# SSD steps of a Mamba-2 / short-conv trunk: decays two half groups ahead, tiles moved between sums, spreads and products, decay subtractions behind the convolutions

## Chip, cores and metric

The kernel runs on one core of a Trainium2 chip. The metric is device time in microseconds (us), the median of several runs; lower is better. One further execution was taken with the hardware profiler, and all rows below come from it.

## What is computed

Two layers, each wrapped by two half-step SwiGLU FFNs, over 256 positions of 1024 channels. Layer 0 mixes with a Mamba-2 SSD block, layer 1 with a short convolution; an RMS norm stands before each part. The change touches the SSD block alone:

```
zxbcdt = h @ w_in                      # z 2048, x 2048, B 4x128, C 4x128, dt 32
xbc = silu(causal_dwconv(xbc, conv_w) + conv_b)      # 4 taps over x, B and C
dt = softplus(dt_raw + dt_bias); a = -exp(a_log)
a_cs = cumsum(dt * a) within chunks of 128
lmat = exp(a_cs[t] - a_cs[s]) for s <= t, else 0
y = (C B^T * lmat) @ (x * dt) + state of the chunk before, decayed
y = y + x * d_skip
g = y * silu(z)
g = g * rsqrt(mean over each of 4 groups of 512 (g*g) + eps) * norm_w
out = g @ w_out
```

All of it is float32 in and out.

## The kernel before, in words

Weights stream from HBM in units of 128 x 1024. `Weights.split` turns each unit into a high part (`whi`, a cast on ACT, L169) and a low part (`wlo`, a subtraction on DVE, L170), and TensorE multiplies high by high, high by low and low by high: three products of 256 columns for every 128 x 128 weight tile in the SSD block (`mm3`, L264 to L266). A weight unit can be used only when its cast and its subtraction are done.

The SSD block's 32 heads are worked as eight half groups of four heads, h = 0 to 7. The string `SSD_STEPS` is the program order of its steps. A letter is the kind, the digits are the half group or group and a part of it:

- `x`: one 128-channel tile of x, eight weight tiles (24 products), then a convolution (`conv_silu`: one ACT instruction L471, three DVE instructions L473) and a SiLU on ACT (L482).
- `z`: one tile of z, 24 products, then SiLU on ACT for the first six tiles (`z00` to `z21`), and for the other ten a Tanh on ACT (L640) and one DVE instruction (L641).
- `d`: the same convolution for B and C of a group; `c`: the products C B^T of a group and their mask (L577 on DVE, L582 on ACT).
- `t`: four transposes of x into PSUM (L648), multiplied by dt on DVE (L656).
- `e`: the decays of a half group: for two of its heads two Relus each on ACT (L668), for the other two two subtractions each on DVE (L670); two Exps over them on ACT (L672, L673), four more Exps for the decay from the chunk before (L677); one DVE multiplication of 128 x 1536 (L680) writes the masked matrix `mt`, which is held twice. It reads `acb`, a broadcast of a_cs loaded by a DMA that ACT issues (L621) two half groups earlier.
- `y`: the sixteen small products of a half group (L693, L698) from `mt` and t's result; then on DVE y + d x (L704) and the gate (L709 or L711), and a Square on ACT (L714, L717), added up on POOL (L718).
- `n`: the group sum (L325) and its inverse root on POOL (L330); `r`: the spread of that root over the partitions by two products (L337), then the norm (L724 on DVE, a cast L282 on ACT, L283 on DVE); `o`: 24 products with w_out into accumulators that stay in PSUM (L746 to L748).

SiLU lies in one activation table, Exp and Tanh in another; ACT loads a table (ACT_TABLE_LOAD) where the kind changes from one instruction to the next.

Program order is not issue order. The Tile framework schedules the built instructions on each engine by its own estimate of times, and the result is fixed when the kernel is built: each engine runs its list strictly in order. `behind(i, first)` adds an edge without a semaphore, so that the scheduler puts `i` after `first`. PSUM tiles of the tag `ps` (all single tiles of x, z, t, y, c, n and r) share four buffers; which tile takes which buffer is also fixed at the build, and the first product into a buffer waits until the tile before it in that buffer has been read.

Of the kernel before, what the change touches and what calls it, by code (L numbers as in the profile page):

```python
# [13 lines left out]
AF = mybir.ActivationFunctionType  # L14
ALU = mybir.AluOpType
# [25 lines left out]
def tile_order():  # L41
# [62 lines left out]

SSD_STEPS = (
# [4 lines left out]
).split()  # L110
SILU_TILES = 6
RELU_HEADS = 2
# [78 lines left out]
def trunk(ctx: ExitStack, tc: tile.TileContext, xT, flat, par, cst, fin, out):  # L191
    nc = tc.nc
    vec, act, pe = nc.vector, nc.scalar, nc.tensor
# [29 lines left out]
    def c(i):  # L223
        return pr[:, i : i + 1]
# [13 lines left out]
    def sb(tag, shape, bufs=2, dt=F32):  # L238
        return tmp.tile(shape, dt, tag=tag, name=nm(tag), bufs=bufs)

    def behind(i, first):

        if first is not None:
            tc.add_manual_dep(
                i.ins, first.ins.name,
                mybir.DependencyInfo(mybir.DependencyClass.NoSync, mybir.DependencyReason.DATA),
                reason="order",
            )
        return i
# [207 lines left out]
    def ssd(nxt):  # L457
# [6 lines left out]
        def conv_silu(dst, u, ct):  # L464

            a = sb("u2", [P, T], 3)

            def w(k):
                return c(C_CW + ct * 4 + k)

            act.activation(a, u, AF.Identity, bias=c(C_CB + ct), scale=w(3))  # L471
            for sh in (1, 2, 3):
                vec.scalar_tensor_tensor(  # L473
                    a[:, sh:], u[:, : T - sh], w(3 - sh), a[:, sh:], op0=ALU.mult, op1=ALU.add
                )
            silu(dst, a)


        exps, silus = [], []

        def silu(dst, src):
            silus.append(behind(act.activation(dst, src, AF.Silu), exps[0] if exps else None))  # L482
# [21 lines left out]
        def bc_conv(g):  # L504
            conv_silu(bT[g], raw[g][:, 0], 16 + g)
            conv_silu(cT[g], raw[g][:, 1], 20 + g)
# [112 lines left out]
        def bcast(h):  # L619
            a = acb[h] = sb("acb", [P, 4, T], 2)  # L620
            nc.scalar.dma_start(a, decays[1][4 * h : 4 * h + 4].partition_broadcast(P))  # L621

        def do_x(h, e):
            if e == 0:
                xh[h] = big.tile([P, 2, T], F32, tag="blk", name=nm("xs"), bufs=KF)
            ps = single()
            run(mm3, [(ps[:, :T], "ssd_in", DI + (2 * h + e) * P)], KD, xn)
            conv_silu(xh[h][:, e], ps[:, :T], 2 * h + e)
# [29 lines left out]
        def do_e(h):  # L658

            g = h // 2  # L660
            a, acs = acb[h], decays[0]
            e = mt[h] = sb("mt", [P, 4, 3, P], 2)
            for q in range(4):
                hd = 4 * h + q
                for ch in range(2):
                    aq, eq, bias = a[:, q, ch * P : (ch + 1) * P], e[:, q, 2 * ch], acs[:, ch, hd : hd + 1]
                    if q < RELU_HEADS:
                        act.activation(eq, aq, AF.Relu, bias=bias, scale=-1.0)  # L668
                    else:
                        vec.tensor_scalar(eq, aq, bias, 0.0, op0=ALU.subtract, op1=ALU.min)  # L670
            r = RELU_HEADS
            behind(act.activation(e[:, :r, 0:3:2], e[:, :r, 0:3:2], AF.Exp, scale=-1.0), silus[-1])  # L672
            behind(act.activation(e[:, r:, 0:3:2], e[:, r:, 0:3:2], AF.Exp), silus[-1])  # L673
            for q in range(4):
                hd = 4 * h + q
                behind(
                    act.activation(e[:, q, 1], a[:, q, P:], AF.Exp, bias=acs[:, 2, hd : hd + 1]),  # L677
                    silus[-1],
                )
            vec.tensor_mul(e, e, cbm[g].unsqueeze(1).broadcast_to([P, 4, 3, P]))  # L680
            if h + 2 < 8:
                bcast(h + 2)
# [56 lines left out]
        def do_o(g, q):  # L739
# [15 lines left out]

        todo = {
            "x": do_x, "z": do_z, "t": do_t, "e": do_e, "p": do_p, "b": do_b, "y": do_y, "n": do_n, "r": group_norm,
            "c": cb_path, "d": bc_conv, "o": do_o,
        }
# [42 lines left out]
    for m in range(KD):  # L802
        if m < 4:
            W.split()
        feed(m, 0, sq=False)
    ffn(0, 0, 1)
    ssd(2)
    ffn(0, 1, 3)
    ffn(1, 0, 4)
# [64 lines left out]
```

## Time and profile before

| | before |
|---|---|
| median of 3 runs | 1050.86 us (1050.17 to 1051.79) |
| the profiled execution's own time | 1051.06 us |
| its span, first to last instruction | 1048.9 us |
| mean granted TensorE clock | 0.998 |
| TensorE busy | 1035.6 us, 99% |
| VectorE (DVE) busy | 782.0 us, 75% |
| ScalarE (ACT) busy | 615.5 us, 59% |
| GpSimd (POOL) busy | 34.2 us, 3% |

A share of busy time is an average over the whole span. The SSD steps run from about 225 to 395 us; the rest is FFNs and the short convolution. What an engine waits for is shown as an idle time and the instruction that ended it.

### The profile page before, as it was taken

How to read it: one execution, taken by the hardware profiler on the slowest of the kernel's cores; microseconds unless marked ns; L12 is line 12 of the kernel's file. 1: busy time of each engine (PE TensorE's matmuls, PEld its weight loads, DVE VectorE, ACT ScalarE, POOL GpSimd, SP SyncE). 2: the span in 40 equal slices, each digit the busy share in tenths (PEclk: the TensorE clock that was granted, in tenths of full speed). 3: DMA queues.
4: the chain of work that ended last, by engine and by line, in shares of the span. 5: the costliest groups of instructions: out<-in, count | busy, mean ns of one | idle time of the engine just before them, and what ended most of it. 6: DMA issues, size and time to landing. Idle time of an engine off the chain costs nothing.

```text
span 1048.9 us, 16814 instructions
## 1 busy us (share of the span) xinstructions
PE 1035.6 (99%) x6468; PEld 921.4 (88%) x6468; DVE 782.0 (75%) x1176; ACT 615.5 (59%) x985; POOL 34.2 (3%) x41
## 2 busy tenths in 40 slices
PE   8999999999999999999999999999999999999997
PEld 6888888899989898888888888888899988888886
DVE  6977766689898878777766777776667788777643
ACT  7655554567688557555544655554454476555543
POOL 0000000130022200000000000000000000000000
PEclk9999999999999999999999999999999999999999
DMA  8655665556555446666555665566555556665661
GB/s 275 219 186 178 197 187 186 172 172 192 183 199 182 148 154 182 190 190 182 184 194 183 181 186 192 185 183 192 187 174 187 182 181 185 188 190 177 198 198 55
DMA packets 55135, 192.96 MB, mean 184 GB/s; under 512 B 6128, under 2 KB 7696, under 8 KB 55056
## 3 DMA queue, kind: packets, MB, share of 16 engines
q1 hardware_dynamic: 53568, 187.15, 57.6%
q10 hardware_dynamic: 1488, 4.75, 1.3%
q8 instruction: 50, 0.82, 0.3%
q14 instruction: 29, 0.24, 0.1%
HBM read 190.80 MB, written 1.08 MB: 183 GB/s over the span
## 4 chain that ended last, share of the span: by engine, by line
PE 96%; DVE 1%; DMA 1%; ACT 1%; issue 0%; SPq 0%; POOL 0%; POOLq 0%; ACTq 0%; DVEq 0%
PE pp L257 31%; PE pp L259 14%; PE ps L257 13%; PE ps L259 6%; PE ps L264 5%; PE ps L265 5%; PE ps L266 5%; PE pp L256 2%; PE ps L414 2%; PE ps L415 2%; PE ps L413 2%; PE pp L746 1%; PE pp L748 1%; PE pp L747 1%; PE pp L266 1%; PE pp L264 1%
## 5 line engine op out<-in xcount | busy, mean ns | idle before, releaser
L170 DVE TENSOR_TENSOR wlo<-raw,whi 128x1024 fp32r<-128x1024 f32 (+2 forms) x361 | 432.1, 1199 | 186.4 <-ACT whi L169 180.1
L169 ACT CAST whi<-raw 128x1024 fp32r<-128x1024 f32 (+2 forms) x361 | 370.5, 1028 | 325.0 <-issue 98.9
L257 PE MATMUL pp<-xhl,whi 128*128 128x512 f32 x1408 | 485.9, 398 | 2.7 <-DVE xhl L295 1.8
L259 PE MATMUL pp<-xhl,wlo 128*128 128x256 f32 x1232 | 346.5, 281 | 0.2
L257 PEld LDWEIGHTS pp<-xhl,whi 128*128 128x128 f32 x1408 | 253.2, 188 | 52.2 <-DVE xhl L295 3.2
L259 PEld LDWEIGHTS pp<-xhl,wlo 128*128 128x128 f32 x1232 | 232.8, 189 | 9.3 <-DVE wlo L170 1.6
L257 PE MATMUL ps<-ac,whi 128*128 128x512 f32 x528 | 185.2, 399 | 0.0
L259 PE MATMUL ps<-ac,wlo 128*128 128x256 f32 x504 | 141.5, 281 | 0.0
L257 PEld LDWEIGHTS ps<-ac,whi 128*128 128x128 f32 x528 | 97.8, 188 | 22.4
L259 PEld LDWEIGHTS ps<-ac,wlo 128*128 128x128 f32 x504 | 95.2, 189 | 1.1
L370 DVE TENSOR_TENSOR t2b<-pp,t2a 128x512 f32<-128x512 f32 x88 | 60.4, 686 | 18.6 <-ACT t2a L370 18.6
L264 PE MATMUL ps<-xn,whi 128*128 128x256 f32 x256 | 73.8, 288 | 0.3 <-DVE u L473 0.3
L265 PE MATMUL ps<-xn,whi 128*128 128x256 f32 x256 | 72.4, 283 | 0.0
L266 PE MATMUL ps<-xn,wlo 128*128 128x256 f32 x256 | 72.4, 283 | 0.0
L370 ACT COPY t2a<-pp 128x512 f32<-128x512 f32 x88 | 51.1, 581 | 32.5 <-PE pp L257 32.5
L378 DVE TENSOR_TENSOR t2b<-t2b,inv 128x512 f32<-128x512 f32 x88 | 60.1, 684 | 0.1
L264 PE MATMUL ps<-xhl,whi 128*128 128x256 f32 x192 | 54.4, 284 | 0.2 <-ACT u L777 0.2
L265 PE MATMUL ps<-xhl,whi 128*128 128x256 f32 x192 | 54.3, 283 | 0.0
L266 PE MATMUL ps<-xhl,wlo 128*128 128x256 f32 x192 | 54.3, 283 | 0.0
L264 PEld LDWEIGHTS ps<-xn,whi 128*128 128x128 f32 x256 | 49.0, 191 | 1.4 <-issue 1.2
L256 PE MATMUL pp<-xhl,wlo 128*128 128x256 f32 x176 | 49.7, 282 | 0.0
L265 PEld LDWEIGHTS ps<-xn,whi 128*128 128x128 f32 x256 | 49.0, 192 | 0.0
(175 smaller groups left out, 1328.6 us busy)
## 6 DMA issues: line engine op xcount, KB each, us to landing
raw<-flat SPq DMA_DIRECT2D x347, 512.0 KB, 3.6
acb<-ad ACTq DMA_DIRECT2D x8, 512.0 KB, 4.6
raw<-flat SPq DMA_DIRECT2D x5, 256.0 KB, 3.1
raw<-flat SPq DMA_DIRECT2D x8, 128.0 KB, 4.1
x<-xT SPq DMA_DIRECT2D x3, 256.0 KB, 5.4
fw<-fin SPq DMA_DIRECT2D x2, 256.0 KB, 4.4
out<-y SPq DMA_DIRECT2D x2, 256.0 KB, 2.0
out<-y ACTq DMA_DIRECT2D x2, 256.0 KB, 2.5
```

Source lines behind the costliest of these rows:

```text
L169: self.nc.scalar.copy(hi[:, :w], r[:, :w])
L170: self.nc.vector.tensor_sub(lo[:, :w], r[:, :w], hi[:, :w].bitcast(F32))
L256: pe.matmul(ps[:, :T], lo, xs[:, 0], start=False, stop=False)
L257: pe.matmul(ps, hi, xs.rearrange("p a t -> p (a t)"), start=first, stop=last)
L259: pe.matmul(ps[:, :T], lo, xs[:, 0], start=False, stop=False)
L264: pe.matmul(ps, hi, xs[:, 0], start=first, stop=False)
L265: pe.matmul(ps, hi, xs[:, 1], start=False, stop=False)
L266: trail.append(pe.matmul(ps, lo, xs[:, 0], start=False, stop=last))
L370: first = act.copy(pb, pp[:, :, T:]), vec.tensor_add(s, pp[:, :, :T], pb)
L378: vec.tensor_mul(s, s, both(inv))
L413: pe.matmul(ps[b], xh, hi, start=False, stop=False)
L414: pe.matmul(ps[b], xh, lo, start=False, stop=False)
```

## The change

A new order of the steps in `SSD_STEPS`, and two further edges for the scheduler. In the string, `e1` stands ahead of `c3`, `e2` ahead of `t2`, and so on, each decay step some tiles earlier than before; `z` and `o` tiles stand between `n` and `r`, and between `r` and `o`, in another way. In the code, the Relus of the decays are put behind the SiLU that was last in program order, and the DVE subtractions behind the convolution that was last in program order (`convs` records the last tap of each).

```
-    "c2 x60 x61 e0 x70 x71 c3 z20 z21 e1 y0 t2 z30 y1 z31 t3 e2 z40 z41 e3 n0 y2 z50 r0 y3 e4 t4 "
-    "o00 z51 t5 e5 o01 o02 o03 n1 y4 t6 z60 r1 e6 z61 y5 t7 z70 e7 y6 z71 o10 o11 n2 o12 y7 o13 r2 "
-    "o20 n3 o21 o22 r3 o23 o30 o31 o32 o33"
+    "c2 x60 x61 e0 x70 x71 e1 c3 z20 z21 y0 e2 t2 z30 y1 e3 t3 z31 z40 y2 e4 n0 t4 z41 z50 y3 e5 r0 "
+    "t5 z51 o00 o01 n1 y4 e6 t6 z60 o02 r1 o03 z61 y5 e7 t7 z70 o10 y6 n2 z71 o11 r2 y7 o12 o13 o20 "
+    "n3 o21 r3 o22 o23 o30 o31 o32 o33"
...
             for sh in (1, 2, 3):
-                vec.scalar_tensor_tensor(
+                i = vec.scalar_tensor_tensor(
                     a[:, sh:], u[:, : T - sh], w(3 - sh), a[:, sh:], op0=ALU.mult, op1=ALU.add
                 )
+            convs.append(i)
             silu(dst, a)
...
-        exps, silus = [], []
+        exps, silus, convs = [], [], []
...
                     if q < RELU_HEADS:
-                        act.activation(eq, aq, AF.Relu, bias=bias, scale=-1.0)
+                        behind(act.activation(eq, aq, AF.Relu, bias=bias, scale=-1.0), silus[-1])
                     else:
-                        vec.tensor_scalar(eq, aq, bias, 0.0, op0=ALU.subtract, op1=ALU.min)
+                        behind(
+                            vec.tensor_scalar(eq, aq, bias, 0.0, op0=ALU.subtract, op1=ALU.min),
+                            convs[-1],
+                        )
```

What the build makes of it is seen in the fixed lists of the engines. Lines after L680 of the changed kernel stand 4 lower than in the one before (L669 is the Relu, L672 the subtraction, L676, L677 and L681 the Exps, L684 the multiplication, L697 and L702 y's products, L708, L713 and L715 y + d x and the gate).

First place: ACT, from the last SiLUs of z to the decays of half group 1 (`mt_288` before, `mt_284` now) and, now, of half group 2 (`mt_295`). Before:

```order
L482 ACTIVATE zs_285_3243<-ps_286_3244 128x256
L169 CAST whi106_3297<-raw106_3127 128x1024
L482 ACTIVATE xs_279_3163<-u2_283_3232 128x256
L482 ACTIVATE zs_285_3243<-ps_287_3276 128x256
L672 ACT_TABLE_LOAD
L672 ACTIVATE mt_288_3308<-mt_288_3308 128x2x2x128
L673 ACTIVATE mt_288_3308<-mt_288_3308 128x2x2x128
L677 ACTIVATE mt_288_3308<-acb_232_2544,acs_225_2469 128x128 x4
L714 ACTIVATE gsq_292_3338<-zs_226_2471 128x256
L621 DMA acb_289_3324<-ad_2467 128x1024
L717 ACTIVATE sq_294_3343<-zs_226_2471 128x256
```

And in the change:

```order
L483 ACTIVATE xs_279_3163<-u2_283_3232 128x256
L669 ACTIVATE mt_284_3238<-acb_232_2544,acs_225_2469 128x128 x4
L677 ACT_TABLE_LOAD
L677 ACTIVATE mt_284_3238<-mt_284_3238 128x2x2x128
L676 ACTIVATE mt_284_3238<-mt_284_3238 128x2x2x128
L681 ACTIVATE mt_284_3238<-acb_232_2544,acs_225_2469 128x128 x4
L483 ACT_TABLE_LOAD
L483 ACTIVATE zs_287_3261<-ps_289_3294 128x256
L622 DMA acb_285_3254<-ad_2467 128x1024
L718 ACTIVATE gsq_292_3338<-zs_226_2471 128x256
L721 ACTIVATE sq_294_3343<-zs_226_2471 128x256
L669 ACTIVATE mt_295_3346<-acb_278_3161,acs_225_2469 128x128 x4
```

The four Relus of half group 1 now stand directly ahead of its table load (before, they stood some 60 rows earlier, among the convolutions); the same holds for half group 0. The last SiLU of z now comes after these Exps, with a table load of its own, and the row that follows the ones shown is the table load for half group 2. The whole list has 17 table loads where it had 15.

Second place: TensorE, from y of half group 2 (`ps_316`) to the tile z41 (`ps_327`), with the semaphores that each row waits for. In the change:

```order
L702 MATMUL ps_316_3521<-mt_295_3346,t2a_298_3369 64x128 x2
L325 MATMUL ps_323_3559<-ones_94,gsq_292_3338 128x2 [waits DVE_49,Pool_49]
L325 MATMUL ps_323_3559<-ones_94,gsq_292_3338 128x2
L649 MATMUL ps_325_3565<-cs_74,xs_259_2877 128x128 [waits DVE_49,PE_49]
L649 MATMUL ps_325_3565<-cs_74,xs_259_2877 128x128 x3
L264 MATMUL ps_327_3572<-xn_187_2197,whi107_3393 128x256 [waits DVE_49]
```

Before, y of half group 2 (`ps_320`) was followed by a whole z tile:

```order
L325 MATMUL ps_318_3555<-ones_94,gsq_292_3338 128x2
L693 MATMUL ps_320_3561<-mt_309_3450,t2a_296_3351 64x256 [waits DVE_49]
L693 MATMUL ps_320_3561<-mt_309_3450,t2a_296_3351 64x256 [waits Activation_49]
L698 MATMUL ps_320_3561<-mt_309_3450,t2a_296_3351 64x128 x2
L693 MATMUL ps_320_3561<-mt_309_3450,t2a_296_3351 64x256 [waits Activation_49] x2
L698 MATMUL ps_320_3561<-mt_309_3450,t2a_296_3351 64x128 x2
L264 MATMUL ps_326_3582<-xn_187_2197,whi108_3430 128x256 [waits DVE_49]
```

In the change the transposes t4 (`ps_325`) are put into the PSUM buffer that y of half group 2 has just filled, and z41 (`ps_327`) into the buffer of t4; so each of the two waits for DVE. The same pattern comes again one half group later: y of half group 3 (`ps_332`), the spread r0 (`ps_339`), the transposes t5 (`ps_348`) in y's buffer, and z51 (`ps_350`) in the buffer of z41.

Third place: DVE in the change, what stands between the reads of the first two of those buffers, y's `ps_316` and t4's `ps_325`:

```order
L708 SCALAR_TENSOR_TENSOR u4_319_3535<-xs_241_2669,pr_73,ps_316_3521 128x256 [waits DVE_49]
L713 TENSOR_TENSOR zs_287_3261<-u4_317_3530,zs_287_3261 128x256 [waits DVE_49]
L713 TENSOR_TENSOR zs_287_3261<-u4_319_3535,zs_287_3261 128x256 [waits DVE_49]
L672 TENSOR_SCALAR mt_321_3541<-acb_296_3362,acs_225_2469 128x128 [waits DMAHW4_49]
L672 TENSOR_SCALAR mt_321_3541<-acb_296_3362,acs_225_2469 128x128 x3
L657 TENSOR_TENSOR t2a_326_3570<-ps_325_3565,dt5_201_2225 128x512 [waits PE_49]
```

And between the reads of the next two, y's `ps_332` and z41's `ps_327`:

```order
L708 SCALAR_TENSOR_TENSOR u4_333_3650<-xs_244_2707,pr_73,ps_332_3641 128x256 [waits DVE_49,PE_49]
L684 TENSOR_TENSOR mt_321_3541<-mt_321_3541,cbm2_175_2031 128x1536 [waits DVE_49,Activation_49]
L715 SCALAR_TENSOR_TENSOR zs_299_3371<-u4_333_3650,zs_299_3371 128x256 [waits DVE_49]
L708 SCALAR_TENSOR_TENSOR u4_335_3656<-xs_244_2707,pr_73,ps_332_3641 128x256
L170 TENSOR_TENSOR wlo110_3594<-raw110_3313,whi110_3593 128x1024 [waits DMAHW1_49,Activation_49]
L642 SCALAR_TENSOR_TENSOR zs_313_3486<-u3_328_3603,ps_327_3572 128x256 [waits Activation_49]
```

So the product of t4's result waits behind two gates and four subtractions, and the second read of y of half group 3 behind the multiplication of half group 4 and a gate.

## Rows read from the trace of the kernel before

**Rows 1.** The page, busy time: engine, us (share of the span), instructions.
```profile
PE 1035.6 (99%) x6468; PEld 921.4 (88%) x6468; DVE 782.0 (75%) x1176; ACT 615.5 (59%) x985; POOL 34.2 (3%) x41
```
**Rows 2.** Waits of TensorE from 225 to 395 us: us in total, times, longest.
```profile
PE ps L693 <- DVE mt L680: 1.7, 2, 1.0
PE ps L337 <- POOL tv L330: 1.1, 1, 1.1
PE pp L746 <- DVE x L753: 0.4, 1, 0.4
PE ps L264 <- DVE u L473: 0.3, 1, 0.3
```
**Rows 3.** Windows: us; PE, PEld, DVE, ACT, POOL busy; granted clock, DMA share, GB/s.
```profile
260.00:283.00 23.00, 23.00 (x193) 22.95 (x192) 19.75 (x34) 14.36 (x24) 0.00 (x0) 1.00 0.58 175
283.00:295.00 12.00, 12.00 (x104) 11.35 (x103) 9.98 (x16) 11.94 (x23) 0.00 (x0) 1.00 0.51 167
300.00:318.00 18.00, 17.34 (x153) 16.33 (x152) 16.56 (x34) 14.69 (x37) 4.73 (x4) 1.00 0.53 185
```
**Rows 4.** Timeline of ACT: start, us, instruction, count, [idle before it].
```profile
283.08 0.41 ACT L482 ACTIVATE xs<-u 128x256 f32<-128x256 f32 x1
283.49 1.28 ACT L672 ACT_TABLE_LOAD   x1
284.79 0.63 ACT L672 ACTIVATE mt<-mt 128x512 f32<-128x512 f32 x1
...
287.12 1.28 ACT L482 ACT_TABLE_LOAD   x1
...
291.81 0.39 ACT L482 ACTIVATE zs<-ps 128x256 f32<-128x256 f32 x1
292.21 1.28 ACT L672 ACT_TABLE_LOAD   x1
...
294.56 1.27 ACT L677 ACTIVATE mt<-acb,acs 128x128 f32<-128x128 f32 x4
...
298.70 1.28 ACT L668 ACTIVATE mt<-acb,acs 128x128 f32<-128x128 f32 x4
299.88 0.62 ACT L673 ACTIVATE mt<-mt 128x512 f32<-128x512 f32 x1
```
**Rows 5.** Timeline of TensorE around y of half group 1 (L693 at 297.70).
```profile
293.13 0.66 PE L648 MATMUL ps<-cs,xs 128*128 128x128 f32 x4
293.54 0.37 PE L264 MATMUL ps<-xn,whi 128*128 128x256 f32 x1
...
297.70 0.65 PE L693 MATMUL ps<-mt,t2a 128*64 128x256 f32 x4 [1.04 <-DVE mt L680]
...
299.15 0.39 PE L264 MATMUL ps<-xn,whi 128*128 128x256 f32 x1
```
**Rows 6.** Timeline of DVE in the stretch of half groups 0 to 3.
```profile
295.89 1.75 DVE L680 TENSOR_TENSOR mt<-mt,cbm 128x1536 f32<-128x1536 f32 x1
...
302.76 0.69 DVE L656 TENSOR_TENSOR t2a<-ps,dt 128x512 f32<-128x512 f32 x1 [0.38 <-PE ps L648]
...
305.76 1.22 DVE L170 TENSOR_TENSOR wlo<-raw,whi 128x1024 fp32r<-128x1024 f32 x1
306.89 0.41 DVE L641 SCALAR_TENSOR_TENSOR zs<-u,ps 128x256 f32<-128x256 f32 x1
...
310.31 0.87 DVE L704 SCALAR_TENSOR_TENSOR u<-xs,pr,ps 128x256 f32<-128x256 f32 x2 [0.97 <-PE ps L698]
311.10 0.75 DVE L709 TENSOR_TENSOR zs<-u,zs 128x256 f32<-128x256 f32 x2
311.77 0.87 DVE L670 TENSOR_SCALAR mt<-acb,acs 128x128 f32<-128x128 f32 x4
```
**Rows 7.** Groups by line, POOL's additions: count | busy us, mean ns | idle before.
```profile
L718 POOL TENSOR_TENSOR gsq<-gsq,sq 128x256 f32<-128x256 f32 x12 | 16.2, 1350 | 105.7 <-ACT sq L717 105.3
```
**Rows 8.** Timeline of DVE, the first subtractions of the decays.
```profile
236.08 0.87 DVE L670 TENSOR_SCALAR mt<-acb,acs 128x128 f32<-128x128 f32 x4 [4.32 <-DMA acb<-ad]
```

## Prediction

> **What bounds the kernel now.** I read the page's busy times first: TensorE is busy 1035.6 of 1048.9 us [rows 1], so a change of order can only take away idle time of TensorE, or add some. Next come TensorE's waits in the SSD stretch: y waits twice for the decay multiplication L680, 1.7 us in all, 1.04 of it before y of half group 1 [rows 2, 5]; a spread waits 1.1 us for POOL; a product waits 0.3 us for a convolution; the 0.4 us at the block's end is not touched. So the most that the order can give back here is 1.7 + 1.1 + 0.3 = 3.1 us. Third, the windows by stage, for what the waits wait for: from 283 to 295 us ACT is busy 11.94 of 12.00 us, where DVE still has 2 us free; from 260 to 283 us ACT had 8.6 us free [rows 3]. ACT is idle 41% of the whole span [rows 1], yet in these 12 us it is the engine that sets the decays. The granted clock is 1.00 in all three windows, which is the level of 2.4 GHz.
>
> **The change, step by step.** Durations are those of the profiled execution, whose own time is 1051.06 us, 0.2 above the median.
>
> *Decay subtractions behind the convolutions.* Before, the first four subtractions held DVE until their broadcast had landed, 4.32 us of idle time [rows 8], and convolutions queued behind them; the product that waited 0.3 us [rows 2] stands there. Now that queue is clear: -0.3.
>
> *y of half group 1.* The Exps of half groups 0 and 1 keep their places behind x, but eight Relus that stood among the convolutions now stand right ahead of them on ACT, where nothing is free. Four Relus hold ACT for 1.18 us, from 298.70 to 299.88 [rows 4]; two sets are 2.36. One SiLU of z moves behind the Exps, which gives 0.40 (291.81 to 292.21 [rows 4]). So the last Exp ends at 295.83 + 1.96 = 297.8 (295.83 is 294.56 + 1.27 [rows 4]), the multiplication of 1.75 us [rows 6] at 299.6, and y starts at about 299.7 where it started at 297.70. TensorE gets there at 296.66 as before, since y, t2 and z30 precede it in both orders [rows 5]. The wait grows from 1.04 to 3.0: **+2.0**.
>
> *y of half group 2.* From 297.8 ACT works off: a table load of 1.28 back to SiLU, that SiLU (0.3), two Squares and a DMA issue (1.0, an estimate from the 0.39 of the SiLU), four Relus 1.18, a load of 1.28, and Exps of 2.33 (284.79 to 287.12) [rows 4]. That ends at 305.2 and its multiplication at 307.0. TensorE gets there at 299.7 + 1.45 (y, 297.70 to 299.15) + 0.41 (transposes, 293.13 to 293.54) + 24 and then 20 products of 0.12, or 306.8 (a tile of 24 products lies between 293.54 and 296.66) [rows 5]. So y waits 0.2. The next weight unit's cast stands behind the same Exps and its subtraction behind the multiplication, ready at 307.0 + 1.1 = 308.1, about 0.3 later than wanted: **+0.5** together.
>
> *y2, t4 and z41 in one buffer.* t4 cannot start before both reads of y, 0.87 us [rows 6], and only the two tiny sums of n0 (some 0.4) are left for TensorE meanwhile: 0.5. Then z41 waits for the product of t4's result, which stands behind two gates and four subtractions: from 311.10 to 312.55 such a row of six took 1.45 us, and the product itself 0.69 [rows 6]. That is 2.1 us from t4's start, less 0.41 for the transposes themselves: 1.7. Together **+2.1** with rounding.
>
> *y3, t5 and z51.* DVE reads y3 in two halves with the multiplication of half group 4 and a gate between them: 0.39 + 1.67 + 0.33 + 0.47 = 2.9 us [rows 6], less some 0.4 of spread products: 2.5. z51 then waits for the read of z41, which stands behind a weight subtraction: 1.13 + 0.41 [rows 6], less 0.41 of transposes: 1.1. **+3.6**.
>
> *The bounds of these two.* Before shows no such buffer wait, so the 5.7 us are worked out from other rows. From below: if TensorE reaches y later than I reckon, more of DVE's queue is done, and half of it goes, 2.9. From above: a row of DVE that waits for ACT in between adds one cast, about 1 us, to each. I take the sums of the rows, since the list on DVE is fixed and every row in it has a measured duration.
>
> *POOL.* The sums n0, n1 and n3 now come close behind the last Square. An addition on POOL lasts 1.35 us in the mean [rows 7]; each sum waits for between none and one of them, so 0 to 4.0 in all. I take **+0.8**, near the lower end, because a whole y or o stands between most of them.
>
> *Waits that go.* The 0.7 us left of the y waits was y3's, now reckoned above with its buffer, and the 1.1 us at the last spread goes, since 24 products now lie between n3 and r3: -1.8. DMA traffic, weight units and the number of products are the same, so nothing else moves.
>
> **The sum.** -0.3 + 2.0 + 0.5 + 2.1 + 3.6 + 0.8 - 1.8 = +6.9 on 1051.06, and 0.2 less for the median: **1057.7 us**.
>
> On the table loads, a row first: ACT begins the next instruction 1.30 us after a load's start (283.49 to 284.79), and the load begins the moment the one before ends (283.08 + 0.41) [rows 4]; so the two added loads are 2.6 us of ACT. The Trainium skill ("ScalarE: Activation LUTs", section "What ACT_TABLE_LOAD costs") has a drain of about 1.38 us beside the load of 1.28, so two added switches would hold ACT 5.3 us, y of half group 2 would come 2.8 us later, and the sum would be 1060.5. The rows show no such drain, so I leave it out.
>
> **Rivals.**
>
> *The decays do come early enough (faster).* If the multiplication of half group 1 ended by 296.66, when TensorE arrives, and the buffers were read in time, the 3.1 us of waits would go: 1047.8. For it: ACT is idle 41% of the span, and the steps are named earlier. Against it: by the rows the multiplication ends at 299.6, 3 us past that point, because the Relus moved to where ACT is full. Chance 0.04.
>
> *The buffer waits are mostly hidden.* ACT is late as forecast, but TensorE, held up once, finds DVE done. Then 4.5 or more of the 5.7 us go: 1053. Against it: a wait inside one buffer starts from y's own end, however late that is. Chance 0.13.
>
> *The order changes nothing that counts.* The waits that go and those that come would have to cancel within 2 us, which needs both the ACT term and one buffer chain to fail. Chance 0.05.
>
> *The clock falls.* The wait before y of half group 1 becomes 3.0 us, three times the longest of this stretch [rows 2]. If TensorE dropped to its level of 1.2 GHz until y of half group 2, up to 7.3 us of work would take up to twice as long; half of that is +3.6: 1061.3. The rows have 1.00 around waits of about 1 us and nothing longer, so they cannot exclude it. Chance 0.06. The Trainium skill ("TensorE: Matmul & The Clock Gate", section "HAM oscillation — how this bites in real kernels") says that idle gaps between products bring the clock back to its lower level; no row here shows it.
>
> **How the numbers follow.** The forecast has 0.72. About 0.2%, or 2 us, is what a measurement of this kernel can tell from no change. The range is 1053.5 to 1061.5: the low end is the sum with half of the buffer waits and none at POOL (6.9 - 2.9 - 0.8 = +3.2), a little lower to take in part of the hidden-buffer case; the high end adds POOL's upper bound (+3.2) and covers the clock's middle. Faster by over 0.2%: 0.04; within: 0.05; slower: 0.91.
>
> **What would show it.** Right: a wait of some 3 us before y of half group 1, ended by L684; 17 table loads; TensorE waiting for DVE before t4, z41, t5 and z51, 0.5, 1.7, 2.5 and 1.1 us; ACT full from 283 to about 318 us; the wait of the last spread gone; everything after the block as before, only later. Wrong: a wait under 2 us before that y says that the Relus cost nothing there; no waits at the transposes says that the buffers were free.

## The result, and the profile after

The changed kernel takes 1058.97 us (median of 4 runs, 1058.57 to 1059.41). The kernel before, run beside it, takes 1051.13 us (1050.17 to 1051.79). The ratio is 1.006, with a 95% interval of 1.0036 to 1.0084: slower, beyond the 0.2% that a measurement can tell. The two medians are 7.8 us apart (0.75%, inside the interval). The profiled run took 1058.84 us with a span of 1056.4 us, 7.5 more than before. The page's busy times of the changed kernel, which answer to [rows 1]:

```profile
PE 1037.9 (98%) x6468; PEld 922.6 (87%) x6468; DVE 782.8 (74%) x1176; ACT 618.4 (59%) x987; POOL 35.0 (3%) x41
```

The same 6468 products are made. ACT has two instructions more, the two table loads. Of the 7.5 us, 5.2 are more idle time of TensorE and 2.3 longer busy time (1037.9 less 1035.6). TensorE's waits from 225 to 405 us in the changed kernel (us in total, times, longest), which answer to [rows 2]; the 0.4 us at the block's end, as before, is left out:

```profile
PE ps L697 <- DVE mt L684: 3.2, 1, 3.2
PE ps L649 <- DVE u L708: 2.9, 2, 2.4
PE ps L264 <- DVE t2a L657: 1.3, 1, 1.3
PE ps L264 <- DVE zs L642: 0.7, 1, 0.7
```

And in TensorE's timeline of the changed kernel (start, us, instruction, count, idle time before it and who ended it): y of half group 1, t4, z41, t5, z51.

```profile
298.85 0.65 PE L697 MATMUL ps<-mt,t2a 128*64 128x256 f32 x4 [3.21 <-DVE mt L684]
...
310.14 0.63 PE L649 MATMUL ps<-cs,xs 128*128 128x128 f32 x4 [0.52 <-DVE u L708]
...
312.11 0.39 PE L264 MATMUL ps<-xn,whi 128*128 128x256 f32 x1 [1.34 <-DVE t2a L657]
...
323.05 0.63 PE L649 MATMUL ps<-cs,xs 128*128 128x128 f32 x4 [2.43 <-DVE u L708]
324.42 0.39 PE L264 MATMUL ps<-xn,whi 128*128 128x256 f32 x1 [0.75 <-DVE zs L642]
...
325.15 0.41 PE L265 MATMUL ps<-xn,whi 128*128 128x256 f32 x1
325.37 0.41 PE L266 MATMUL ps<-xn,wlo 128*128 128x256 f32 x1
...
328.53 0.28 PE L264 MATMUL ps<-xn,whi 128*128 128x256 f32 x1
328.65 0.28 PE L265 MATMUL ps<-xn,whi 128*128 128x256 f32 x1
```

All five waits stand where the prediction put them; the ones that it had before y of half group 2 and at POOL's sums are not there. The last four rows show something else: products that came every 0.12 us come every 0.21 us for a while. The windows of that stretch say why (us; PE, PEld, DVE, ACT, POOL busy; granted clock, DMA share, GB/s):

```profile
322.00:324.00 2.00, 0.63 (x4) 0.42 (x4) 2.00 (x5) 1.40 (x5) 0.83 (x1) 1.00 0.00 0
324.00:326.00 2.00, 1.58 (x8) 1.58 (x9) 2.00 (x5) 1.01 (x3) 0.63 (x1) 0.70 0.42 78
326.00:328.00 2.00, 2.00 (x11) 2.00 (x11) 2.00 (x9) 1.53 (x5) 0.74 (x1) 0.50 0.81 223
```

TensorE's clock fell to 0.50, its level of 1.2 GHz, after the waits before t5 and z51. Fifteen products from 324.94 to 328.14 us took 3.20 us instead of 1.80, a loss of 1.4 us. The sum of the rows is +2.17 (3.21 instead of 1.04) + 5.04 (the four waits) + 1.4 (clock) - 2.1 (the waits of 0.3, 0.7 and 1.1 us that went) = +6.5 of the 7.5 us. The last 1.0 us is for the most part two products that start only when DVE has made the low part (`wlo`) of their weight unit. The two subtractions in DVE's timeline, and the two products in TensorE's with the one before the second:

```profile
305.73 1.77 DVE L170 TENSOR_TENSOR wlo<-raw,whi 128x1024 fp32r<-128x1024 f32 x1
307.56 0.39 PE L266 MATMUL ps<-xn,wlo 128*128 128x256 f32 x1
...
313.64 1.22 DVE L170 TENSOR_TENSOR wlo<-raw,whi 128x1024 fp32r<-128x1024 f32 x1
314.49 0.28 PE L265 MATMUL ps<-xn,whi 128*128 128x256 f32 x1
314.91 0.39 PE L266 MATMUL ps<-xn,wlo 128*128 128x256 f32 x1
```

The subtractions end at 307.50 and 314.86, and the products start 0.06 and 0.05 us later; the second stands 0.42 us behind the product before it, where 0.12 is the usual step. That makes 0.3 to 0.4 us for each, an estimate. Such short waits stand in no list of waits above.

Rows that name an instruction as the end of a wait do not tell why it came so late, nor whether the parts add up. The experiments ask that.

### The profile page after: what moved, and what is told of

The parts are those of the page before. It is cut to its first block, busy times and chain, and to the rows that moved or that the text cites. A ratio compares the mean times of both kernels' runs of the same rounds, so it can differ in the third digit from the quotient of the medians.

```text
span 1056.4 us, 16828 instructions
## 1 busy us (share of the span) xinstructions
PE 1037.9 (98%) x6468; PEld 922.6 (87%) x6468; DVE 782.8 (74%) x1176; ACT 618.4 (59%) x987; POOL 35.0 (3%) x41
## 4 chain that ended last, share of the span: by engine, by line
PE 93%; ACT 3%; DVE 1%; DMA 1%; issue 1%; SPq 0%; POOL 0%; ACTq 0%; DVEq 0%; POOLq 0%
PE pp L257 31%; PE pp L259 14%; PE ps L257 13%; PE ps L259 6%; PE ps L264 5%; PE ps L266 5%; PE ps L265 4%; PE pp L256 2%; PE ps L415 2%; PE ps L413 2%; PE ps L414 2%; PE pp L750 1%; PE pp L751 1%; PE pp L752 1%; PE pp L266 1%
## 5 line engine op out<-in xcount | busy, mean ns | idle before, releaser
L259 PE MATMUL pp<-xhl,wlo 128*128 128x256 f32 x1232 | 346.5, 281 | 0.4 <-DVE wlo L170 0.2
L266 PEld LDWEIGHTS ps<-xn,wlo 128*128 128x128 f32 x256 | 49.7, 194 | 0.9 <-DVE wlo L170 0.9
```

The costliest lines, as they stand in the source:

```text
L259: pe.matmul(ps[:, :T], lo, xs[:, 0], start=False, stop=False)
L266: trail.append(pe.matmul(ps, lo, xs[:, 0], start=False, stop=last))
```

## The experiments

**Theory A** is the prediction's: the Relus on a full ACT, and buffers shared between a y and the tile behind it, are prices of their own that add up. **Theory B** says that the decays, named two half groups ahead, put DVE's list in the wrong order, and that the shared buffers are only where TensorE meets that. Further rivals stand in the expectations. All times are medians, and each ratio is to runs of the kernel before on the same chip.

### The order alone, and the edges alone

```diff
 (order_only: the changed kernel, and)
-behind(act.activation(eq, aq, AF.Relu, bias=bias, scale=-1.0), silus[-1])
+act.activation(eq, aq, AF.Relu, bias=bias, scale=-1.0)
-behind(vec.tensor_scalar(eq, aq, bias, 0.0, op0=ALU.subtract, op1=ALU.min), convs[-1])
+vec.tensor_scalar(eq, aq, bias, 0.0, op0=ALU.subtract, op1=ALU.min)
 (edges_only: both edges, and the SSD_STEPS of the kernel before)
```

> The new order of steps with none of the new edges. Theory A (the parts of the changed kernel's loss add up: y of half group 1 +2.2, the four waits before t4, z41, t5 and z51 +5.0, the lower clock after them +1.5, a late weight unit +0.3, waits that went -2.1): without the edge on the Relus they stand among the convolutions again, so the wait before y of half group 1 falls from 3.2 to 1.0 to 1.3 us and the rest stays; 1051.1 + 0.2 + 5.0 + 1.5 + 0.3 - 1.8 = 1056.3, and the clock still falls after z51. Rival C (the loss is the Relu edge's, since ACT is full there and all that comes later is late because of it): 1050 to 1052, and the waits before t4, z41, t5 and z51 shrink with the one before y of half group 1.

> The old order of steps with both new edges. Theory A: the wait before y of half group 1 is about 3.3 us (eight Relus now on a full ACT; it was 1.04), the 0.3 us before a product goes, and the two waits of the group sums and the spread in the last quarter (0.7 and 1.1) stay; no shared buffers, clock 1.00 throughout; 1051.1 + 2.3 - 0.3 = 1053.1, less whatever of y3's 0.7 us the delay takes up: 1052.4 to 1053.1. Rival C (the edge is the whole loss): 1057 to 1059. Rival D (the edge costs nothing, since the scheduler finds the Relus another place): 1050.5 to 1051.3.

The order alone took 1058.3 us (1.0067, 1.0049 to 1.0084), 2 us over what theory A gave. The wait before y of half group 1 was 1.3 us as expected and the four others were as in the changed kernel, but the median is only 0.7 us lower than the changed kernel's (the profiled runs, 1057.4 and 1058.84, are 1.4 apart). The clock fell here too, to 0.55 and 0.60 from 322 to 326 us. This kernel also lacks the edge of the convolutions, which is tried by itself below.

The edges alone took 1052.86 us (1.0008, 0.9996 to 1.002), the time that theory A gave, but not in its way: the clock, which was to stay at 1.00, fell. TensorE's timeline of that run has the longer wait, and products every 0.21 us behind it:

```profile
299.31 0.65 PE L697 MATMUL ps<-mt,t2a 128*64 128x256 f32 x4 [3.37 <-DVE mt L684]
...
301.60 0.41 PE L265 MATMUL ps<-xn,whi 128*128 128x256 f32 x1
301.81 0.41 PE L266 MATMUL ps<-xn,wlo 128*128 128x256 f32 x1
```

Of its 12 runs, eleven have a mean granted clock of 0.996 to 0.998 and take 1052.1 to 1054.1 us; one has 1.000 and takes 1050.56. So a fall of the clock goes with about 2.3 us here (1052.86 less 1050.56), an estimate that rests on that one run; it has no trace, so whether its wait was as long is not known. The waits of y3 and of a product (0.7 and 0.3 us) have gone from the traced run. Rival C, which wanted 1050 to 1052 for the order and 1057 to 1059 for the edges, is out: by the medians the order costs 7.2 us by itself, the edges 1.8 (the interval of their ratio takes in 1), and both together 7.8.

### The four tiles in buffers of their own

```diff
-            pt = single()
+            pt = pair()[:, 0] if h in (4, 5) else single()
...
-            py = single()
+            py = pair()[:, 0] if h in (2, 3) else single()
```

> The changed kernel, but y of half groups 2 and 3 and the transposes t4 and t5 get the four PSUM banks that the output accumulators take up only later, so none of the four shares a buffer with the tile behind it. Theory A: the four waits go (-5.0) and with them the fall of the clock (-1.5): 1059.0 - 6.5 = 1052.5. Rival B (DVE is behind by then, because the decays' multiplications stand earlier in its list, and the shared buffer is only where TensorE happens to meet that): nothing is gained, 1057 to 1059; the same 4 to 6 us stand before y of half group 3, before a product that reads a wlo (L170), or before the first products of o, and DVE's list ends the stretch at the same time as in the changed kernel.

1063.9 us (1.0116, 1.0099 to 1.0133): nothing was gained, 5 us were lost. TensorE's waits in this run:

```profile
PE ps L697 <- DVE mt L684: 3.2, 1, 3.2
PE ps L266 <- DVE wlo L170: 2.3, 1, 2.3
PE pp L751 <- DVE gn L283: 2.3, 1, 2.3
PE pp L697 <- DVE mt L684: 1.3, 1, 1.3
PE ps L697 <- DVE zs L642: 0.4, 1, 0.4
```

No transposes wait any more, but TensorE waits for the next things that DVE owes: a weight unit, the norm of r0, the decays of half group 3. That is 6.3 us behind y of half group 1, where the changed kernel had 5.04. Theory A's second part falls. The clock was low twice here, at 0.51 and 0.64 from 300 to 304 us and at 0.50 to 0.83 from 326 to 338; the changed kernel has one short fall. So some 1.3 of the 5 us are waits, and the rest goes with the clock (an estimate, the difference of the two): shared buffers or not, the waits for DVE come to much the same.

### The last third of the order alone

```diff
 ... y3 e4 t4 o00 z51 t5 e5 o01
-o02 o03 n1 y4 t6 z60 r1 e6 z61 y5 t7 z70 e7 y6 z71 o10 o11 n2 o12 y7 o13 r2 o20 n3 o21 o22 r3 o23
+n1 y4 e6 t6 z60 o02 r1 o03 z61 y5 e7 t7 z70 o10 y6 n2 z71 o11 r2 y7 o12 o13 o20 n3 o21 r3 o22 o23
```

> The kernel before, with the new order only from n1 on (half groups 4 to 7 and the output tiles between the sums, spreads and norms), without the edges. Theory A and rival B alike: the waits of the last quarter (0.7 before a group sum or y, 1.1 before the last spread) fall to 0.3 or less and nothing is added, 1051.1 - 1.5 = 1049.6, so the gain of the change was real and was in the string's last third. Rival E (those two waits only move to the sums, which now come close behind the last addition on POOL): 1050.8 to 1051.5.

1055.19 us (1.0039, 1.0025 to 1.0052), with runs from 1052.64 to 1059.93. Both expectations missed on the slow side. The profiled run is the fastest of them, so what the others add to it is in no trace. TensorE waits three times for POOL, 3.3 us, 2.6 of it before n2 (its row in TensorE's timeline):

```profile
352.24 0.61 PE L325 MATMUL ps<-ones,gsq 128*128 128x2 f32 x4 [2.61 <-POOL gsq L718]
```

The two additions that n2 waits for took POOL 5.03 us, where the same two took 1.56 in the changed kernel. POOL's rows of this run and of the changed kernel, one line each:

```profile
347.16 5.03 POOL L718 TENSOR_TENSOR gsq<-gsq,sq 128x256 f32<-128x256 f32 x2 [14.85 <-ACT sq L717]
```

```profile
353.31 1.56 POOL L722 TENSOR_TENSOR gsq<-gsq,sq 128x256 f32<-128x256 f32 x2 [10.99 <-ACT sq L721]
```

So the wait of 1.1 us before the last spread, which went in the changed kernel, was not a gain of this part of the order by itself: here it goes too, but 3.3 us of waits for POOL take its place. In the changed kernel POOL has the time: its two additions start 5.1 us before n2's products (353.31 and 358.44), here only 2.5 us before TensorE is ready for them (347.16, and 352.24 less 2.61). Why the Squares come sooner there is not shown. A delay of TensorE by itself is not enough: edges_back, below, is held up for 3.37 us before y of half group 1 and still waits 1.9 us for POOL at two sums. One reason why runs of such kernels lie far apart is shown next.

### The decays back, and the decays alone

```diff
 (decays_back: order_only with e1 to e5 one half group ahead, as before)
-e1 c3 z20 z21 y0 e2 t2 z30 y1 e3 t3 z31 z40 y2 e4 n0 t4 z41 z50 y3 e5 r0 t5 z51 o00
+c3 z20 z21 e1 y0 t2 z30 y1 e2 t3 z31 z40 e3 y2 n0 t4 z41 z50 y3 e4 r0 t5 z51 e5 o00
 (decays_early: the kernel before with e1 to e5 two half groups ahead)
-c3 z20 z21 e1 y0 t2 z30 y1 z31 t3 e2 z40 z41 e3 n0 y2 z50 r0 y3 e4 t4 o00 z51 t5 e5
+e1 c3 z20 z21 y0 e2 t2 z30 y1 e3 z31 t3 z40 z41 n0 y2 e4 z50 r0 y3 e5 t4 o00 z51 t5
```

> The new order without the new edges (as in order_only), but with the decay steps e1 to e5 back behind the tiles where the kernel before has them, one half group ahead instead of two. In the built lists t4, z41, t5 and z51 then each get a buffer of their own. Theory B, now sharper (the decays two half groups ahead put a multiplication of 1.75 us and its wait for ACT ahead of the reads, gates and weight subtractions that TensorE needs next; all else in the new order is harmless): the wait of y3's read and all four waits before t4, z41, t5 and z51 go, the clock stays at 1.00 between 320 and 330 us, and what is left are y of half group 1 (1.0) and some waits of sums for POOL (1 to 3, as in tail_alone): 1050 to 1053, from 1058.3. Rival F (the tiles of z and the transposes, moved between the y steps, are the cause): 1056 to 1059, with the same four waits.

> The kernel before, where only the decay steps e1 to e5 are moved to the places that they have in the change; all other steps and the code as before. Theory B: DVE and ACT get behind as in the change, TensorE waits 3 to 6 us more between 300 and 330 us, at a product that reads a wlo (L170), at the first product of o or at a z tile, and perhaps a second or two of lower clock behind it: 1054 to 1058. Rival F: nothing but a shift of waits, 1050.5 to 1052.

With the decays back, the new order takes 1053.77 us (1.0025, 1.0011 to 1.004) instead of 1058.3. The decays alone, moved early in the old order, take 1056.51 us (1.0046, 1.003 to 1.0063), 5.5 us over the kernel before on the same chip; TensorE waits there 1.9 us for the read of a z tile and 1.9 us for weight subtractions, and the clock is at 0.50 from 322 to 324 us. Theory B forecast the second; the first lies 0.8 us over its upper end. The waits before t4, t5 and z51 are gone as it said, and the clock is at 1.00 from 320 to 330 us, but z41 still waits 1.02 us for DVE's read of a z tile. Rival F missed both. DVE's waits of the changed kernel from 300 to 330 us, and then those of decays_back from 300 to 335, show what is different:

```profile
DVE u L708 <- PE ps L702: 6.2, 3, 3.2
DVE mt L684 <- ACT mt L681: 0.7, 1, 0.7
```

```profile
DVE wlo L170 <- ACT whi L169: 1.0, 1, 1.0
DVE mt L680 <- ACT mt L677: 0.6, 1, 0.6
DVE u L704 <- PE ps L698: 0.5, 1, 0.5
```

In the changed kernel DVE itself stands idle for 6.2 us, for y. It is not too slow; its list is in the wrong order. DVE's timeline around y of half group 3 in the changed kernel:

```profile
320.03 0.48 DVE L708 SCALAR_TENSOR_TENSOR u<-xs,pr,ps 128x256 f32<-128x256 f32 x1 [3.16 <-PE ps L702]
320.43 1.75 DVE L684 TENSOR_TENSOR mt<-mt,cbm 128x1536 f32<-128x1536 f32 x1
322.09 0.42 DVE L715 SCALAR_TENSOR_TENSOR zs<-u,zs 128x256 f32<-128x256 f32 x1
322.43 0.47 DVE L708 SCALAR_TENSOR_TENSOR u<-xs,pr,ps 128x256 f32<-128x256 f32 x1
322.82 1.22 DVE L170 TENSOR_TENSOR wlo<-raw,whi 128x1024 fp32r<-128x1024 f32 x1
```

And in decays_back:

```profile
317.79 1.22 DVE L170 TENSOR_TENSOR wlo<-raw,whi 128x1024 fp32r<-128x1024 f32 x1
...
319.26 1.22 DVE L170 TENSOR_TENSOR wlo<-raw,whi 128x1024 fp32r<-128x1024 f32 x1
...
320.84 0.87 DVE L704 SCALAR_TENSOR_TENSOR u<-xs,pr,ps 128x256 f32<-128x256 f32 x2
```

With late decays, DVE splits the next weight units while TensorE is still busy, and is there when y is done; TensorE has tiles to go on with. With early decays, the read of y stands ahead of the weight units, so DVE waits 3.16 us for TensorE. Then the multiplication of a half group that is not needed yet (1.75 us) goes ahead of the second read and the weight unit, and TensorE waits for DVE. Each engine idles in turn.

The runs of decays_back lie between 1051.68 and 1058.81 us; the profiled one took 1056.56 and shows one reason; no other run of this kernel has a trace. Before DVE's first subtraction, and before the product behind it:

```profile
239.11 0.87 DVE L670 TENSOR_SCALAR mt<-acb,acs 128x128 f32<-128x128 f32 x4 [7.57 <-DMA acb<-ad]
```

```profile
242.57 0.36 PE L264 MATMUL ps<-xn,whi 128*128 128x256 f32 x1 [3.55 <-DVE u L473]
```

The row of the kernel before has 4.32 us [rows 8], and 0.3 us of a product's wait; the traces of order_only, tail_alone and decays_early have 4.2 to 4.4 us. So the broadcast's DMA landed some 3 us later in this run than in the four others, and all that DVE has behind that subtraction waited with it.

### The edge of the convolutions

```diff
 (back_conv: decays_back, and)
 (conv_edge: the kernel before, and)
-vec.tensor_scalar(eq, aq, bias, 0.0, op0=ALU.subtract, op1=ALU.min)
+behind(vec.tensor_scalar(eq, aq, bias, 0.0, op0=ALU.subtract, op1=ALU.min), convs[-1])
```

> As decays_back, and with the change's edge of the subtractions behind the convolutions (not the one of the Relus). Theory B: the edge takes away the 0.3 us before one product and may bring the read of z31 or z40 forward by up to 1.5 us, so 0.3 to 1.5 us under decays_back. Rival G (the edge does nothing): the same time as decays_back within 0.5 us.

> The kernel before with the edge of the subtractions behind the convolutions alone. Theory H (in the kernel before, DVE's first subtraction stands ahead of convolutions and waits 4.3 us for the broadcast by DMA, 7.6 us in the profile of decays_back, where a product then waited 3.5 us; how late that DMA lands differs from run to run): the idle time of L672 for the DMA goes, the median falls by no more than 0.7 us, to 1050.2 to 1051.0, and no run lies over 1053, while the kernel before has runs to 1056. Rival: the scatter has another cause and stays, with runs of 1054 to 1056.

back_conv takes 1051.08 us (0.9998, 0.9987 to 1.0009), 2.7 under decays_back: more than theory B's 1.5, and rival G is out. conv_edge takes 1050.35 us (0.9978, 0.9964 to 0.9992), faster than the kernel before by 0.22%, which is just more than can be told from no change; the medians are 1.4 us apart (1051.78 before), twice the fall of 0.7 that theory H allowed, though the time lies in its range. Its twelve runs lie between 1049.61 and 1051.06; of the 29 runs of the kernel before beside it (1050.39 to 1057.86), 11 lie over 1053. None does with the edge, as theory H had it; its rival is out. DVE's wait for the broadcast is gone from its trace; its first wait of that stretch, at 232.90 us, is 1.71 us for ACT's part of a convolution.

So one of the two edges is a gain, and the whole change hides it.

### The edge of the Relus

```diff
 (relu_free: the changed kernel, and)
-behind(act.activation(eq, aq, AF.Relu, bias=bias, scale=-1.0), silus[-1])
+act.activation(eq, aq, AF.Relu, bias=bias, scale=-1.0)
 (edges_back: the changed kernel, and the steps of decays_back)
```

> The changed kernel without the edge of the Relus; its order of steps and the edge of the subtractions stay. Theory A (the parts add up): the wait before y of half group 1 falls from 3.2 to about 1 us and the time by 2.2, to 1056.8. Theory B (DVE is behind for its decays anyway, so a TensorE that comes 2 us earlier to y of half groups 2 and 3 waits the longer there): under 1 us of gain, 1058.0 to 1059.0, and 1 to 2 us more than in the changed kernel before t4, z41, t5 and z51 or in lower clock.

> The changed kernel with both edges, and only the decay steps e1 to e5 back behind the tiles where the kernel before has them. Theory B: of the loss of 7.8 us only the wait before y of half group 1 (3.3 us, part of it taken up by y of later half groups) and a fall of the clock behind it stay, as in edges_only, which took 1.8 us more than the kernel before: 1051.1 + 1.8 = 1052.9, with 1051 to 1054 as the bounds (no fall of the clock; a wait of n1 for POOL besides). Theory A (the early decays are not what matters): 1057 to 1059.

relu_free takes 1058.3 us (1.0059, 1.0037 to 1.008): 0.7 us of gain for 2.4 us less of wait (3.2 to 0.8). The time is theory B's, but not its reason: the four waits grew only from 5.04 to 5.22 us. What took the gain is the clock, which fell twice in this run, at z51 as in the changed kernel and also after the waits of 0.52 and 1.33 us before t4 and z41. The windows of relu_free:

```profile
308.00:310.00 2.00, 1.01 (x7) 1.01 (x8) 2.00 (x4) 2.00 (x8) 0.77 (x1) 0.93 0.60 201
310.00:312.00 2.00, 2.00 (x11) 2.00 (x10) 2.00 (x4) 2.00 (x7) 2.00 (x1) 0.50 0.04 10
```

edges_back takes 1054.54 us (1.0021, 1.0006 to 1.0037), with 3.4 us before y of half group 1, the clock at 0.50 from 300 to 302 us, and 1.3 us before n1. That is 0.5 over theory B's upper bound of 1054, and 4.4 under the changed kernel, by the decays alone; theory A's 1057 to 1059 is out. With back_conv there are four kernels that differ in two things only, all with the edge of the convolutions (medians; the kernel before took 1050.97 us beside back_conv, 1051.78 beside edges_back and relu_free, 1051.13 beside the changed kernel):

| | Relus free | Relus behind SiLUs |
|---|---|---|
| decays one half group ahead | 1051.08 | 1054.54 |
| decays two half groups ahead | 1058.30 | 1058.97 |

The edge of the Relus costs 3.5 us where nothing else is late and 0.7 where the decays are; the early decays cost 7.2 and 4.4. In these times the two are not a sum, and the traces say why: in this block the clock fell never in back_conv, once in edges_back and in the changed kernel, and twice in relu_free. Take 1.4 us, the price measured above, off the profiled time for each fall: 1050.43, 1054.67, 1057.55 and 1058.84 (back_conv, edges_back, relu_free, changed) become 1050.4, 1053.3, 1054.8 and 1057.4. By this estimate, from one profiled run of each kernel, the edge costs 2.8 and 2.7 us and the early decays 4.3 and 4.2. So the two prices nearly add up, as theory A had it of the Relus, and it is the falls of the clock that do not.

### Versions that give POOL time

```diff
 (sums_later: back_conv, and)
-o00 o01 n1 y4 e6 t6 z60 o02 r1 o03 z61 y5 e7 t7 z70 o10 y6 n2 z71 o11 r2
+o00 o01 y4 e6 t6 z60 n1 o02 r1 o03 z61 y5 e7 t7 z70 o10 y6 z71 n2 o11 r2
 (best: sums_later, and)
-y3 e4 r0 t5 z51 e5 o00 o01
+y3 r0 t5 e4 z51 o00 e5 o01
```

> As back_conv, but the sums n1 and n2 stand one or two tiles later, so that POOL's additions (up to 5.0 us for two in tail_alone, where n2 waited 2.6 us) are done when TensorE comes to them. If POOL is what holds tail_alone: no wait of L325 for POOL over 0.7 us, no fall of the clock, 1048.5 to 1050, under the kernel before. If the additions on POOL only get slower in turn: 1051 to 1055, with runs that differ by several us, as in tail_alone.

> As sums_later, and e4 and e5 one tile later again (e4 behind t5, e5 behind o00), so that DVE has y of half group 3 read and gated before their multiplications. Theory B: the wait of 0.8 us before y of half group 4 goes, 0.3 to 0.8 us under sums_later: 1049.7 to 1050.3. If that wait only moves to another y: 1050.5.

sums_later takes 1050.48 us (0.9988, 0.9977 to 1.0), not to be told from the kernel before, and between the ranges of its two expectations; no sum waits more than 0.2 us for POOL in it, and y of half group 4 waits 0.8 us instead. The second takes 1049.94 us (0.9981, 0.9967 to 0.9996), inside theory B's range and without that wait: just under the kernel before, and not to be told from conv_edge. TensorE's waits in it:

```profile
PE ps L697 <- DVE mt L684: 1.0, 1, 1.0
PE ps L264 <- DVE zs L642: 0.5, 1, 0.5
PE ps L325 <- POOL gsq L722: 0.5, 1, 0.5
PE pp L750 <- DVE x L757: 0.4, 1, 0.4
PE ps L337 <- POOL tv L330: 0.3, 1, 0.3
```

These waits still come to 2.7 us. So the new order with its decays late and its sums later is worth no more than the edge alone.

## Why the prediction was right, and where its steps were not

- **Time and sign.** 1057.7 was forecast and 1058.97 measured, inside the range. The cause in outline, that the decays hold up the work TensorE needs next, holds.
- **y of half group 1, +2.0.** The wait grew by 2.17 us, as worked out from ACT's rows. The median of relu_free is only 0.7 us lower, because its clock fell once more; with the falls priced, the term is 2.7 us.
- **y of half group 2 and the late weight unit, +0.5.** No wait stands before that y in the changed kernel's trace, but the weight unit behind the multiplication was late as forecast, by 0.3 to 0.4 us. A second late unit, at 314.91 us, was not in the sum.
- **y2, t4 and z41 in one buffer, and y3, t5 and z51; 0.5, 1.7, 2.5 and 1.1.** Measured: 0.52, 1.34, 2.43 and 0.75. The waits are the forecast's, its reason is not. The step that failed is "in one PSUM buffer": own_buffers took the sharing away and kept 6.3 us of waits, where 5.04 had stood. The rows that the prediction counted on DVE between two reads are the cause, whichever buffer is read.
- **POOL, +0.8.** No sum waits more than 0.2 us for POOL in the changed kernel. In tail_alone three sums wait 3.3 us, inside the bounds of 0 to 4.0. So the price exists, but whether it falls due hangs on how long before a sum its Squares are done (5.1 or 2.5 us before n2) and on how long the additions take (1.56 or 5.03 us for the same two), which the prediction put at a mean.
- **Waits that go, -1.8, and -0.3 for the convolutions.** They went. But in tail_alone the 1.1 us of the last spread go and 3.3 us at the sums come, and the edge of the convolutions was sized on one profile: it is worth 2.7 us in back_conv and 0.22% in conv_edge. That the difference is the DMA's, which landed late in one of five traces, fits the narrower runs of both kernels with the edge, but of the slow runs without the edge only that one was traced.
- **The clock, a rival with 0.06.** It fell, and cost 1.4 us in the profiled run, but behind t5 and z51, not behind y of half group 1. In edges_only and edges_back it fell behind that y, after 3.37 us, as the rival had it, and in own_buffers after 3.19. It should have stood in the sum.
- **The table loads.** From the start of an added load to the next instruction there are 1.29 us in the changed kernel (300.40 to 301.69), so the drain of the Trainium skill ("ScalarE: Activation LUTs", section "What ACT_TABLE_LOAD costs") does not show here either. The rows on ACT:

```profile
300.40 1.28 ACT L677 ACT_TABLE_LOAD   x1
301.69 0.63 ACT L677 ACTIVATE mt<-mt 128x512 f32<-128x512 f32 x1
```

That the sum came out so near is luck: what it lacked (1.4 us of clock, some 0.3 for the second weight unit) and what it had too much (0.8 for POOL, 0.7 for the buffers) are of one size.

## What to carry to other kernels

Before a step is moved earlier, look at what then stands behind it on each in-order engine: work that is not due yet delays the reads and weight splits that TensorE needs next, and both engines may idle in turn though neither is full. A wait that names a buffer is explained only when the buffer is taken away and the wait goes with it. Keep a first use of a DMA's data behind work whose inputs are already there; what that saves shows in the scatter of the runs, not in one profile. Before two costs are called no sum, count the falls of the clock in each trace.

## What the runs showed of the hardware

- **Clock.** The changed kernel's profile keeps 1.00 through an idle time of 3.21 us, while own_buffers falls to 0.51 after one of 3.19 us (its row is below), edges_only to 0.56 after one of 3.37 us, and relu_free to 0.50 after waits of 0.52 and 1.33 us between short pieces of work. Of edges_only's twelve runs one has a mean clock of 1.000, so the same list of instructions can go either way (how long its wait was in that run is not known). The Trainium skill ("TensorE: Matmul & The Clock Gate", section "HAM oscillation — how this bites in real kernels") says that idle gaps between products bring the clock back to its lower level: the rows agree that they can, and show that the length of a single gap does not decide it.

```profile
298.91 0.65 PE L697 MATMUL ps<-mt,t2a 128*64 128x256 f32 x4 [3.19 <-DVE mt L684]
```

- **POOL beside DVE.** The same two additions took 5.03 us in tail_alone and 1.56 in the changed kernel. In tail_alone DVE was busy 6.00 of 6.00 us there, first with a weight subtraction and a multiplication that read two SBUF tiles each:

```profile
347.06 1.21 DVE L170 TENSOR_TENSOR wlo<-raw,whi 128x1024 fp32r<-128x1024 f32 x1
348.19 1.75 DVE L680 TENSOR_TENSOR mt<-mt,cbm 128x1536 f32<-128x1536 f32 x1
```

The Trainium skill ("SBUF — State Buffer", section "Who interferes with whom") says that a DVE instruction with two inputs in SBUF contends with a GpSimd instruction that reads SBUF. The rows fit that. So does the changed kernel: in its 1.56 us (353.31 to 354.87) DVE had one product that reads PSUM, of 0.68 us, and then stood idle for 0.92 us. But no run changes the DVE work alone to show it.
